# TensorE's queue in the first stage: written order or scheduler's order, in a streaming layer with short convolution and gated delta rule

## The chip, the cores and the metric

The kernel runs on one core of a Trainium2 chip. A core has TensorE (PE, matrix products; its weight loads are shown as PEld), VectorE (DVE), ScalarE (ACT), GpSimd (POOL) and SyncE (SP, which issues the DMAs here). Each engine works through a queue of its own; semaphores tie the queues together. The metric is the device time of one execution in microseconds, as the median of several. Every profile below is of one execution, taken by the hardware profiler.

## The reference

One layer over 4096 new tokens of a prompt (and 32 of a running stream), model width 1024, float32. All tokens are normalised and projected to 4096 columns and 8 gate columns. Mixer A is a gated convolution of width 3 over 512 channels. Mixer B is a gated delta rule with 4 heads of 128, whose state S runs through the whole sequence in chunks:

```python
def hybrid_layer(x, buf_a, buf_qkv, s0, ln_pre, w_in, ...):
    h = rmsnorm(x, ln_pre)
    proj = jnp.einsum('btd,dp->btp', h, w_in)
    b_a, c_a, x_a, z_a, qkv, z_g, a_dec, b_beta = jnp.split(proj, splits, axis=-1)
    conv_a, new_buf_a = causal_dwconv(c_a * x_a, buf_a, conv_a_w)
    y_a = b_a * conv_a * jax.nn.silu(z_a)
    qkv = silu(causal_dwconv(qkv, buf_qkv, conv_qkv_w));  q, k, v = split(qkv)
    q, k = l2norm(heads(q)), l2norm(heads(k));  g, beta = ...
    # gated_delta_rule, by chunks of tokens:
    #   a_mat = strict_lower(kbeta k^T * decay);  t_mat = (I + a_mat)^-1
    #   u = t_mat (v beta);  w = t_mat (kbeta exp(g))
    #   per chunk: v_new = u - w S;  o = (q exp(g)) S + attn v_new
    #              S = S exp(g_last) + k_dec^T v_new
    y_g = rmsnorm_head(o) * silu(z_g)
    return x + rmsnorm_post(concat(y_a, y_g) @ w_out)
```

## The kernel before

The work has three stages. In the first, the 4096 tokens go through in 16 blocks of 256 (two chunks of 128 each), and all of mixer B is done. In the second, mixer A's projections follow in a scheme with fewer products (a_pairs), and in the third the output projection (tiles pjo, go, ro). The change is in the first stage.

**One block of the first stage** has eight pairs of projections on TensorE, in the order c4, c6, c0, c2, c8, c10, z0, z2 (tiles pj_c, pj_z; k, q, v and the gate Z of mixer B). A pair is 48 matmuls (each product in three f16 parts, so 384 a block). A pair's result is evacuated by ScalarE, convolved by VectorE (L436, six instructions) and goes through silu on ScalarE. Between the pairs stand the small pieces:

- norm_qk: transposes of q and k (tile gt, L77), squares on ScalarE (L468), and from them kd on VectorE (L471).
- gram: products of k with k and q (tile gq), evacuated by VectorE to M and at (L490, L491). The 32x32 blocks of M's diagonal go through DRAM: lad (L497) and back to la (L536).
- subst: the triangular inverse of these 32x32 blocks. VectorE starts it (L539 to L541), GpSimd multiplies la by it (L546) and makes 31 steps of a product and a subtraction (L550, L551), VectorE transposes the result (L556), and 16 DMAs on SP spread it to Tc (L560).
- merge, a generator in five pieces: px (M x Tc, tile m), then the products with U, a transpose, and two more products, that put the 64- and 128-wide inverse U together (VectorE L608, ScalarE L620 to L632).
- rec_a and rec_b, generators, once per chunk: a transpose of v (ot), rk and rq (S times k and q; R by VectorE L654, o by ScalarE), rv (U times R; vn by ScalarE L667), rS (S by VectorE L674), mo (o by VectorE L687), then squares on ScalarE (L691), `so` on VectorE (L693, L694), its power -1/2 on GpSimd (L137), the scaling of o (L696, L697), its transposes om and the DMA of mixer B's result.
- gates of the next block (ggate, gcs), and for the second stage prep_a (w_in's columns by DMA L205, VectorE L206, ScalarE L749, GpSimd L750 to L762, DMA out) and prep_t (GpSimd, ScalarE).

**What sets the order.** The program is written by slots: block `gi` has slots from `16*gi` on, two to a pair of projections, and each piece is put into a slot by at_slot. Pieces of a block's merge and recurrence stand up to 44 slots behind the block's first, that is in the next block's pairs and the one after. These pieces are written under high_priority(1500) (the helper `first`). The tile framework's scheduler then makes a queue for each engine by its own times, the priorities and the data that instructions need from each other. On TensorE one thing more holds: the helper class Ordered (its lines L58 to L66) gives, while `on` is set, every matmul and transpose an order dependence on the one written before it:

```python
def queue(self, i):
    ins = getattr(i, "ins", i)
    if self.on and self.last is not None:
        tc.add_manual_dep(ins, self.last.name, ... NoSync ..., reason="order")
    self.last = ins
    return i
```

`T.on` is set from the second block on and taken away when the first stage's slots are done and the second stage's first products are written. Merge's pieces stand at slots 26 and 28 to 31 of their block, the second chunk's recurrence at 31 to 44.

Of the kernel before, what the change touches and what calls it, by code (L numbers as in the profile page):

```python
# [49 lines left out]
def hybrid_kernel(  # L50
# [28 lines left out]
    T = Ordered()  # L79
# [369 lines left out]
    def pair(b, kind, c0):  # L449
        n = b["n"]  # L450
        if kind == "z":
            return z_pair(b, c0)
        if kind == "v":
            return qkv_pair(b, c0, b["v"][:, c0 - 8:c0 - 6, :n])
        h0 = c0 % 4
        return qkv_pair(b, c0, b["qk"][:, h0:h0 + 2, 0 if kind == "k" else 1, :n])
# [253 lines left out]
    def setup_block(b):  # L710
        b["nch"] = b["n"] // b["C"]
        b["qk"] = tl([P, NH, 2, NB1], F32, "qk", 3, b["id"])
        if b["s"]:
            b["v"], b["zg"] = (te([P, NH, NS], F32, x, 1, "s") for x in ("vs", "zgs"))
        else:
            b["v"], b["zg"] = (tl([P, NH, NB1], F32, x, 2, b["id"]) for x in ("v", "zg"))
        b["hist_new"] = te([P, 12, 3], F32, "hists" if b["s"] else "hist", 2 if b["s"] else 3, b["id"])
        b["ss"] = te([P, 2, 2, NH], F32, "ss", 2, b["id"])[:b["C"], :b["nch"]]
        nb = b["C"] // 32
        b["lad"] = dp.tile([2, NH, 4, 32, 32], F32, tag=f"lad{nb}", bufs=2, name=f"lad{b['id']}")[:b["nch"], :, :nb]  # L720
        b["kd"], b["M"], b["at"], b["rec"] = [], [], [], {}
# [12 lines left out]
    def prep_a():  # L734


        i, half = divmod(wa["next"], 2)
        if i >= len(pairs):
            return
        wa["next"] += 1  # L740
        ct = pairs[i][0]
        if not half:
            yield from scaled((ct, ct + 1))
            return
        (a11, a12), (a21, a22) = ((w[:, 0:4], w[:, 4:8]) for w in wa["w"])

        def out(k, src):
            hl = te([P, 2, 4, P], F16, "hl", 4, f"{i}_{k}")
            A.activation(hl[:, 0], src, AF.Copy)  # L749
            G.tensor_tensor(hl[:, 1], src, hl[:, 0], ALU.subtract)  # L750
            dma(wad[i][:, k], hl)

        out(0, a11)
        out(1, a12)
        out(2, a22)
        G.tensor_tensor(a22, a21, a22, ALU.add)
        out(3, a22)
        G.tensor_tensor(a21, a11, a21, ALU.subtract)
        out(5, a21)
        G.tensor_tensor(a11, a22, a11, ALU.subtract)  # L760
        out(4, a11)
        G.tensor_tensor(a12, a12, a11, ALU.subtract)  # L762
        out(6, a12)
# [25 lines left out]
    def prep_t(i):  # L789

        j, k = divmod(i, 4)
        s, d = (te([P, D], F32, "xt", NXT, f"{x}{i}").bitcast(F16).rearrange("p (q x n) -> p q x n", q=4, x=2)
                for x in ("ts", "td"))
        t = te([P, NB1], F32, "hl", 4, f"tt{i}")
        for q in range(4):
            dma(s[:, q], hTd[j][:, q // 2, q % 2, :, k])
        sums(G, *([(v[:, q, 0], v[:, q, 1]) for q in range(4)] for v in (s, d)), t)
        dma(hTt[j][:, :, :, k], d)
# [64 lines left out]
    def at_slot(i, fn, *a):  # L863
        slots.setdefault(i, []).append(lambda: fn(*a))

    def run_slot(i):
        for fn in slots.pop(i, ()):
            fn()
# [6 lines left out]
    def ends(gen):  # L875
        for _ in gen:
            pass

    def finish(p, s0):

        n = p["nch"]
        ra = [rec_a(p, c) for c in range(n)]
        rb = [rec_b(p, c) for c in range(n)]
        mg = merge(p)
        if n == 1:
            for i, g in ((19, ra[0]), (20, ra[0]), (23, mg), (24, ra[0]), (25, ra[0]), (25, rb[0])):
                at_slot(s0 + i, first, next, g, None)
            at_slot(s0 + 30, ends, rb[0])
            at_slot(s0 + 30, out_state, p)
            return  # L890
        for i, g in ((24, ra[0]), (26, ra[0]), (26, mg), (28, mg), (29, mg), (30, mg), (31, mg), (31, ra[1]),
                     (32, ra[0]), (34, ra[0]), (34, rb[0]), (36, ra[1]), (38, ra[1]), (39, rb[0]),
                     (40, ra[1]), (40, rb[1]), (44, rb[1])):
            at_slot(s0 + i, first, next, g, None)
        if p["last"]:
            at_slot(s0 + 41, out_state, p)

    def first_group(grp):

        for b in grp:  # L900
            setup_block(b)
            if b["s"]:
                b["hist"] = te([P, 12, 3], F32, "hists", 2, "i")
                state[1] = te([P, NH, P], F32, "hl", 4, "s0")
                dma(state[1], state_gdn[0, 0].rearrange("h k v -> k h v"))
        for si, (kind, c0) in enumerate(steps):
            if si == 4:
                in_turn([gates(b) for b in grp])
                for b in grp:
                    decays(b)  # L910
            for kd_, c_ in steps[:si + 1 + (AH if si >= AS else 0)]:
                ct = (28 if kd_ == "z" else 16) + c_
                if ct not in W:
                    prep_b(ct)
            if kind != "z":
                init_hist(smp, 16 + c0)
            for b in grp:
                ends(pair(b, kind, c0))
            if si == 6:
                xprep(groups[1][0])  # L920
            if si in (4, 5):
                for b in grp:
                    if si - 4 < b["nch"]:
                        stage1(b, si - 4)
            if si == 5:
                for b in grp:
                    rnorms(b)
                    subst(b)
            if si == 7:
                in_turn([gates(groups[1][0])])  # L930

    prevs = []
    for gi, grp in enumerate(groups):
        b, s0 = grp[-1], 16 * gi
        if gi == 0:
            first_group(grp)
            for p in grp:
                finish(p, s0)
        else:
            T.on = True  # L940
            setup_block(b)
            b["hist"] = prevs[-1]["hist_new"]
            at_slot(s0 + 7, first, norm_qk, b, 0, 0)
            at_slot(s0 + 8, first, norm_qk, b, 1, 0)
            at_slot(s0 + 10, first, norm_qk, b, 0, 1)
            at_slot(s0 + 11, first, gram, b, 0)
            at_slot(s0 + 11, first, norm_qk, b, 1, 1)
            at_slot(s0 + 12, first, gram, b, 1)
            at_slot(s0 + 12, first, rnorms, b)
            at_slot(s0 + 12, first, subst, b)  # L950
            if gi + 1 < len(groups):
                nx = groups[gi + 1][0]
                g = gates(nx)
                at_slot(s0 + 2, xprep, nx)
                at_slot(s0 + 9, next, g)
                at_slot(s0 + 10, next, g)
                at_slot(s0 + 13, ends, g)
            finish(b, s0)
            for si, (kind, c0) in enumerate(steps):
                ps = pair(b, kind, c0)  # L960
                next(ps)
                run_slot(s0 + 2 * si)
                ends(ps)
                run_slot(s0 + 2 * si + 1)
                if si == 3:
                    for _ in range((1 <= gi <= 13) + (gi in (4, 7, 10))):

                        p = prevs[-1]
                        with tc.issue_after(p["subst_end"]):
                            pa = prep_a()  # L970
                            if next(pa, 0) is None:
                                at_slot(s0 + 11, next, pa)
                                at_slot(s0 + 13, ends, pa)
                    if gi in (5, 6, 8, 9, 11, 12, 13, 14):
                        with tc.issue_after(prevs[-1]["subst_end"]):
                            prep_t((5, 6, 8, 9, 11, 12, 13, 14).index(gi))
        if gi + 1 < len(groups):
            decays(groups[gi + 1][0])
        for b in grp:
            if b["last"]:  # L980
                out_hist(b)
        prevs = grp
# [408 lines left out]
```

## Time and profile before

| | us |
|---|---|
| median of 3 runs | 2454.54 (2454.03 to 2456.37) |
| profiled execution | 2458.1 |
| its span | 2456.4 |
| granted TensorE clock, mean | 0.942 |

| engine | busy us | share of the span |
|---|---|---|
| PE | 2150.5 | 88% |
| PEld | 1725.1 | 70% |
| DVE | 1549.1 | 63% |
| POOL | 1335.7 | 54% |
| ACT | 984.2 | 40% |

The profile tells for each instruction its start, its duration, its engine and line, the tiles that it writes and reads, and, in brackets, how long its engine was idle before it and what ended that. The stages lie at 0 to about 1420 us (first), to 2092 (second) and to 2456 (third). A stretch's table of windows shows the busy time of every engine in it with the number of instructions, the granted clock, the DMA engines' share and GB/s.

### The profile page before, as it was taken

The page shows a single profiled execution, that of the slowest core. Times are in us where ns is not written, and L with a number is a line of the kernel's source. Part 1 is how long each engine was busy: PE and PEld are TensorE (multiplying, and loading weights), DVE is VectorE, ACT ScalarE, POOL GpSimd, SP SyncE. Part 2 cuts the span into 40 slices and gives each one's busy share as a digit, 9 for nine tenths or more (in the row PEclk, how much of TensorE's full clock was granted, in tenths as well). Part 3 has the DMA queues.
Part 4 walks back from the last instruction along what each step waited for, and adds up shares of the span by engine and source line. Part 5 has one row for each costly group of instructions (what it writes and reads, how often), then busy time and mean ns, then how long its engine had stood idle before and what let it go on. Part 6 is the DMA issues. An engine that isn't in the chain of part 4 may idle for free. (4 is left out here: it accounts for less than half of the span.)

```text
span 2456.4 us, 48167 instructions
## 1 busy us (share of the span) xinstructions
PE 2150.5 (88%) x18626; PEld 1725.1 (70%) x18626; DVE 1549.1 (63%) x3720; ACT 984.2 (40%) x2513; POOL 1335.7 (54%) x1750
## 2 busy tenths in 40 slices
PE   4667988788888888888989988999999999999998
PEld 3446877677677777777877877878888888544443
DVE  4786766666767686667666654565657456466652
ACT  4454555455545554555555411112221112233331
POOL 3434653657565766477675440274575441476663
PEclk9778999899899989999999999999999999999999
DMA  6344332433333334324241432412121104344432
GB/s 122 45 108 85 81 96 62 87 91 104 78 88 103 95 89 91 102 80 102 73 125 55 130 133 99 158 53 87 44 76 55 52 27 137 117 131 141 150 129 78
DMA packets 257198, 230.81 MB, mean 94 GB/s; under 512 B 111576, under 2 KB 196376, under 8 KB 256968
## 3 DMA queue, kind: packets, MB, share of 16 engines
q1 hardware_dynamic: 256968, 227.73, 33.1%
q8 instruction: 146, 2.39, 0.4%
q14 instruction: 84, 0.69, 0.1%
HBM read 133.09 MB, written 76.74 MB: 85 GB/s over the span
## 5 line engine op out<-in xcount | busy, mean ns | idle before, releaser
L74 PEld LDWEIGHTS <-w 128*128 128x128 f16 x6528 | 640.3, 103 | 139.8 <-POOL w L729 18.4
L74 PE MATMUL pj_c<-hhi,w 128*128 128x256 f16 x3072 | 566.7, 285 | 10.6 <-ACT u L430 10.6
L74 PE MATMUL pj_c<-hlo,w 128*128 128x256 f16 x1536 | 437.8, 285 | 0.0
L74 PEld LDWEIGHTS <-w_a 128*128 128x128 f16 x2880 | 268.0, 98 | 69.1 <-issue 36.0
L74 PEld LDWEIGHTS <-opm 128*128 128x128 f16 x1536 | 149.2, 98 | 176.2 <-issue 0.8
L551 POOL TENSOR_TENSOR lt<-lt 128x112 f32<-128x112 f32 (+29 forms) x496 | 229.2, 462 | 37.8
L550 POOL TENSOR_TENSOR lt<-la,lt 128x112 f32<-128x112 f32 (+29 forms) x496 | 215.0, 433 | 37.3
L436 DVE SCALAR_TENSOR_TENSOR qk<-u,cw,qk 128x256 f32<-128x256 f32 x384 | 217.7, 611 | 23.9 <-ACT qk L434 23.8
L74 PE MATMUL pja<-op,w_a 128*128 128x256 f16 x1536 | 189.7, 273 | 12.3 <-DVE w L1034 5.6
L74 PE MATMUL pj_z<-hhi,w 128*128 128x256 f16 x1024 | 197.9, 291 | 2.0 <-ACT u L430 2.0
L74 PE MATMUL ga<-op,w_a 128*128 128x256 f16 x1152 | 146.4, 274 | 18.4 <-DVE w L1034 11.9
L74 PE MATMUL pj_z<-hlo,w 128*128 128x256 f16 x512 | 148.7, 290 | 0.0
L546 POOL TENSOR_TENSOR la<-la,lt 128x1024 f32<-128x1024 f32 x16 | 37.7, 2355 | 156.4 <-DVE lt L541 103.4
L74 PE MATMUL pjo<-w_o,opm 128*128 128x512 f16 x528 | 118.5, 379 | 0.0
L74 PE MATMUL ro<-w_o,opm 128*128 128x512 f16 x504 | 113.4, 379 | 0.0
L74 PE MATMUL go<-w_o,opm 128*128 128x512 f16 x504 | 113.1, 379 | 0.0
L137 POOL TENSOR_TENSOR oss<-oss,mhalf 128x2 f32<-128x2 f32 (+1 forms) x17 | 50.0, 2941 | 114.7 <-DVE oss L1280 114.7
L1034 DVE TENSOR_TENSOR w<-pja,w 128x256 f32<-128x256 f32 x152 | 61.8, 420 | 72.0 <-PE pja L74 69.9
L750 POOL TENSOR_TENSOR hl<-xtw,hl 128x512 f16<-128x512 f32 x56 | 68.9, 1248 | 61.2 <-ACT hl L749 61.2
L137 POOL TENSOR_TENSOR r<-ss,mhalf 128x16 f32<-128x16 f32 x16 | 49.0, 3060 | 94.9 <-DVE ss L509 80.4
L74 PE MATMUL gq<-qk 128*128 128x256 f32 x256 | 70.2, 410 | 33.2 <-ACT jk L468 31.9
L769 ACT ACTIVATE op<-tsc 128x512 f16<-128x512 f32 x48 | 30.2, 630 | 168.1 <-POOL tsc L775 96.4
(649 smaller groups left out, 4716.3 us busy)
## 6 DMA issues: line engine op xcount, KB each, us to landing
xt<-in_x_prompt_dram SPq DMA_DIRECT2D x32, 512.0 KB
mx<-mxd SPq DMA_DIRECT2D x16, 1024.0 KB
op<-hTd SPq DMA_DIRECT2D x30, 512.0 KB
xtw<-in_w_in_dram SPq DMA_DIRECT2D x28, 512.0 KB
wad<-hl SPq DMA_DIRECT2D x56, 256.0 KB
gB<-gd SPq DMA_DIRECT2D x16, 516.0 KB
hTd<-hhi SPq DMA_DIRECT2D x16, 512.0 KB
hTd<-hlo SPq DMA_DIRECT2D x16, 512.0 KB
```

Of the source, the lines that this page charges most:

```text
L74: return self.queue(nc.tensor.matmul(*a, **k))
L137: G.tensor_tensor(y, x, mhalf[:x.shape[0], :x.shape[-1]], ALU.pow)
L436: V.scalar_tensor_tensor(d, u[:, i, j:j + n], cw[:, j, c0 + i:c0 + i + 1], d, ALU.mult, ALU.add)
L546: E.tensor_tensor(la, la, bc(rl, 1, 32), ALU.mult)
L550: E.tensor_tensor(tm, bc(la[:, j, j + 1:32], 2, w), bc(lt[:, j, 0:w], 1, r), ALU.mult)
L551: last = E.tensor_tensor(lt[:, j + 1:32, 0:w], lt[:, j + 1:32, 0:w], tm, ALU.subtract)
L750: G.tensor_tensor(hl[:, 1], src, hl[:, 0], ALU.subtract)
L769: A.activation(d[i][0], t, AF.Copy)
L1034: V.tensor_tensor(dst, p, src, ALU.add)
```

## The change

One line in the loop over the blocks: the written order of TensorE's queue is no longer asked for. The slots remain as the order in which the program is written, and the pieces under `first` keep their priority.

```diff
@@ -937,7 +937,7 @@
             for p in grp:
                 finish(p, s0)
         else:
-            T.on = True
+            pass
             setup_block(b)
             b["hist"] = prevs[-1]["hist_new"]
             at_slot(s0 + 7, first, norm_qk, b, 0, 0)
```

All engines' queues come out differently. Names carry the block: m7 is the tile of merge of block 7, so6_1 the `so` of block 6's second chunk, pj8_c10 a projection of block 8.

TensorE in block 8's projections, before: rk and rq of block 7's first chunk, both halves of px and gt in one run, inside the pair c10.

```order
L74 MATMUL pj8_c10_10028<-hhi8_8537,w21_26_1441 128x256
L74 MATMUL rk7_0_10053<-S6_1_9905,qk7_8411 128x128 x4
L74 MATMUL rq7_0_10062<-S6_1_9905,qk7_8411 128x128 x4
L74 MATMUL m7_10073<-Tc7_9276,M7_0_9087 32x32 x4
L74 MATMUL m7_10073<-Tc7_9276,M7_1_9173 32x32 x4
L74 MATMUL m7_10073<-Tc7_9276,M7_0_9087 32x32 x4
L74 MATMUL m7_10073<-Tc7_9276,M7_1_9173 32x32 x4
L77 MATMUL gt18_0_10097<-ident_63,qk8_9462 128x128 x4
L74 LDWEIGHTS w22_27_1444
L74 MATMUL pj8_c10_10028<-hhi8_8537,w22_27_1444 128x256
```

TensorE after: the first half of px, in the pair c8.

```order
L74 MATMUL pj8_c8_9875<-hlo8_8538,w18_25_1196 128x256
L74 MATMUL m7_10073<-Tc7_9276,M7_0_9087 32x32 x4
L74 MATMUL m7_10073<-Tc7_9276,M7_1_9173 32x32 x4
L74 LDWEIGHTS w19_25_1197
L74 MATMUL pj8_c8_9875<-hhi8_8537,w19_25_1197 128x256
```

TensorE after: the second half of px, 28 projection matmuls later, in the pair c10 among the gram products of block 8.

```order
L74 MATMUL pj8_c10_10028<-hhi8_8537,w22_27_1444 128x256
L74 MATMUL gq08_0_10149<-qk8_9462 128x256
L74 MATMUL m7_10073<-Tc7_9276,M7_0_9087 32x32 x4
L74 MATMUL m7_10073<-Tc7_9276,M7_1_9173 32x32 x4
L74 MATMUL gq08_0_10149<-qk8_9462 128x256
L74 MATMUL gq18_0_10154<-qk8_9462 128x256 x2
```

The two halves of px are apart now, the first 20 to 26 projections earlier, and rk and rq stand over 100 projections earlier.

GpSimd around the end of block 7's substitution, before: the second `so` of block 6 (so6_1) stands behind the last step and other work.

```order
L551 TENSOR_TENSOR lt7_9199<-lt7_9199 128x8
L750 TENSOR_TENSOR hl4_0_9817<-xtw10_8799,hl4_0_9817 128x512
L750 TENSOR_TENSOR hl4_1_9821<-xtw10_8799,hl4_1_9821 128x512
L750 TENSOR_TENSOR hl4_2_9825<-xtw11_8807,hl4_2_9825 128x512
L542 MEMSET lt8_10249 128x256
L756 TENSOR_TENSOR xtw11_8807<-xtw11_8807 128x512
L544 MEMSET lt8_10249 32x8 x4
L758 TENSOR_TENSOR xtw11_8807<-xtw10_8799,xtw11_8807 128x512
L137 TENSOR_TENSOR so6_1_9916<-so6_1_9916,mhalf_100 128x4
```

GpSimd after: so6_1 among the steps.

```order
L550 TENSOR_TENSOR lt7_9199<-la7_9198,lt7_9199 128x56
L551 TENSOR_TENSOR lt7_9199<-lt7_9199 128x56
L550 TENSOR_TENSOR lt7_9199<-la7_9198,lt7_9199 128x48
L137 TENSOR_TENSOR so6_1_9916<-so6_1_9916,mhalf_100 128x4
L551 TENSOR_TENSOR lt7_9199<-lt7_9199 128x48
L550 TENSOR_TENSOR lt7_9199<-la7_9198,lt7_9199 128x40
L551 TENSOR_TENSOR lt7_9199<-lt7_9199 128x40
```

The second `so` stands six steps ahead of the substitution's end instead of behind it. In the other blocks it stands behind step 22 to 30 of 31.

## Rows read from the trace of the kernel before

**Rows 1.** Windows: us, busy PE, PEld, DVE, ACT, POOL, clock, DMA share, GB/s
```profile
267.00:1340.00 1073.00, 920.90 (x8562) 799.28 (x8561) 730.86 (x1874) 579.16 (x1581) 670.50 (x1137) 0.92 0.35 89
518.00:597.00 79.00, 70.15 (x665) 61.50 (x663) 54.31 (x137) 44.00 (x122) 58.84 (x96) 0.94 0.31 90
566.80:571.00 4.20, 4.15 (x31) 3.43 (x32) 4.20 (x8) 0.37 (x2) 2.66 (x2) 0.50 0.31 106
2092.00:2456.00 364.00, 356.28 (x1717) 168.26 (x1716) 191.66 (x336) 116.55 (x259) 207.72 (x122) 1.00 0.38 125
```

**Rows 2.** Waits: engine, line, waited for: us in total, times, longest
```profile
POOL so L137 <- DVE so L694: 61.3, 13, 18.8
...
PE rv L74 <- DVE R L654: 52.3, 7, 12.2
...
PE gq L74 <- ACT jk L468: 31.9, 13, 4.6
...
PE m L74 <- DMA Tc<-la: 31.0, 11, 4.3
```

**Rows 3.** Timeline, 518 to 598: start, duration, engine, line, out<-in, [idle <-releaser]
```profile
518.33 0.19 DVE L541 TENSOR_TENSOR lt<-lt,bl 128x32 f32<-128x32 f32 x1
...
556.49 0.69 DVE L556 STREAM_TRANSPOSE la<-lt 128x256 f32<-128x256 f32 x1 [1.59 <-POOL lt L551]
...
562.25 0.69 PE L74 MATMUL m<-Tc,M 32*32 32x32 f32 x16
566.85 1.03 PE L74 MATMUL m<-Tc,M 32*32 32x32 f32 x16 [3.92 <-DMA Tc<-la]
...
575.65 1.13 PE L74 MATMUL gq<-qk 128*128 128x256 f32 x4 [1.74 <-ACT jk L468]
...
579.24 1.09 PE L77 MATMUL gt<-ident,qk 128*128 128x128 f32 x4 [2.46 <-DVE at L491]
...
585.28 1.99 PE L74 MATMUL gq<-qk 128*128 128x256 f32 x8
...
597.64 0.19 DVE L541 TENSOR_TENSOR lt<-lt,bl 128x32 f32<-128x32 f32 x1
```

**Rows 4.** Timeline, the first and the last L541 of 14
```profile
266.92 0.19 DVE L541 TENSOR_TENSOR lt<-lt,bl 128x32 f32<-128x32 f32 x1
...
1339.65 0.19 DVE L541 TENSOR_TENSOR lt<-lt,bl 128x32 f32<-128x32 f32 x1
```

**Rows 5.** Timeline of VectorE, a block with w_in's columns
```profile
425.89 0.19 DVE L541 TENSOR_TENSOR lt<-lt,bl 128x32 f32<-128x32 f32 x1
...
460.41 1.32 DVE L206 TENSOR_TENSOR xtw<-xtw,lnp 128x1024 f32<-128x1024 f32 x1 [9.02 <-DMA xtw<-in_w_in_dram]
...
462.87 1.11 DVE L654 SCALAR_TENSOR_TENSOR R<-rk,sm,R 128x128 f32<-128x128 f32 x4
...
476.07 0.68 DVE L556 STREAM_TRANSPOSE la<-lt 128x256 f32<-128x256 f32 x1
```

**Rows 6.** Timeline, the second chunk's R and rv
```profile
539.41 0.27 PE L74 MATMUL pj_c<-hhi,w 128*128 128x256 f16 x1
...
542.91 1.11 DVE L654 SCALAR_TENSOR_TENSOR R<-rk,sm,R 128x128 f32<-128x128 f32 x4
...
544.65 1.06 PE L74 MATMUL rv<-R,U 128*128 128x128 f32 x8
```

**Rows 7.** Timeline, the second chunk's mo, S and `so`, and GpSimd's 25th step
```profile
551.40 0.28 POOL L550 TENSOR_TENSOR lt<-la,lt 128x56 f32<-128x56 f32 x1
...
552.55 1.06 PE L74 MATMUL mo<-vn,at 128*128 128x128 f32 x8
...
557.06 1.08 DVE L674 SCALAR_TENSOR_TENSOR S<-S,E,rS 128x128 f32<-128x128 f32 x4
...
560.66 0.65 DVE L693 TENSOR_TENSOR so<-so,sm 128x4 f32<-128x4 f32 x1 [1.35 <-ACT at L691]
...
563.07 1.01 POOL L137 TENSOR_TENSOR so<-so,mhalf 128x4 f32<-128x4 f32 x1
```

## The prediction

> **What bounds the kernel now.** I read the profile by stretches first. In the first stage's steady part TensorE is busy 920.9 of 1073 us at a granted clock of 0.92, in the last stage 356.3 of 364 at 1.00 [rows 1]. The last stage is full and the change doesn't touch it, so a gain must come out of the first, where some 150 us of idle time and the low clock lie. Second, the table of waits: what TensorE waits for there is R of the recurrence (L654), the squares of norm_qk (L468) and the Tc that the substitution sends through DRAM (L560) [rows 2]. None is large by itself, so I followed one block in the timeline.
>
> It closes a loop [rows 3]. The substitution of a block starts on VectorE with L541 at 518.33 and ends with the transpose L556 at 557.18, 38.9 us later. Tc goes out; the first products of merge (px) start at 562.25, 5.1 us after L556, and the second px wait for the rest of Tc until 566.85 (3.9 us of idle TensorE). In TensorE's written order these px stand ahead of the next block's gram products, and so the last gq is at 587.27, 30.1 us after L556. From there M, the diagonal's way through DRAM and back, and L541 at 597.64 take 10.4. Nothing of the next substitution can start earlier, and none of the three legs has slack: 38.9 + 30.1 + 10.4 = 79.3. The loop runs 13 times from 266.92 to 1339.65 [rows 4], 82.5 us a turn. Six turns are like this one. In the seven others w_in's columns are prepared, L206 waits in VectorE's queue for its DMA, R and L556 stand behind it, and L541 to L556 takes up to 50.9 us (425.89 to 476.75) [rows 5].
>
> So the stage ends when the loop has turned, and what the change is worth is: by how much it shortens L556 to the last gq, less what it adds inside the substitution.
>
> **The change part by part.** *TensorE, L556 to the last gq.* Counted in projection matmuls from a block's start, the first half of px moves from 264 to about 238, the second half stays at 264 or goes to 280, the gq move from 288 and 312 to 262 to 312, gt from 192 and 216 to 103, and the first rk/rq from 264 to 139 to 170. So px no longer waits for all of Tc in a row: while the second half's DMA is under way there are 26 or more projections to run, and gt and rk are gone from this stretch. The walk, with the durations of the rows: one projection is (544.65 - 539.41)/48 = 0.109 us, from the first behind rq to rv [rows 6]. Between the first px and the last gq stand 73 of them, 8.0 us; px's second half 1.0, one gt 1.1, sixteen gq twice 1.1 and 2.0, 4.2 [rows 3], the gates' products an estimated 0.8 and the first products with U an estimated 0.9 (32 small ones; px's 32 take 0.7 and 1.0): 16.0. The first px still come at L556 + 5.1, since the DMA sets that, and last 0.7. After an idle stretch of that kind TensorE runs at half clock: 0.50 in the 4.2 us behind the wait for Tc [rows 1], which loses 2.1. Sum: 5.1 + 0.7 + 16.0 + 2.1 = 23.9 instead of 30.1: **-6.2 a turn**. Bounds: -8 if the clock holds; -3 if the waits for the squares and for M's buffers (1.7 and 2.5 in this block) both come back in full.
>
> *GpSimd.* The rsqrt of the second chunk's norm (`so`, L137) took its turn after the 31 steps of the substitution; it now stands behind step 22 to 30. It takes 1.0 us [rows 7], all of it on the loop: **+1.0**. Some 18 steps of prep_t get ahead of later substitutions; at GpSimd's mean of 670.5/1137 = 0.6 us [rows 1] that is 11 us over 13 turns: **+0.8**, between 0 and 1.
>
> *Is `so` there in time?* In this block mo ends at 553.61, 35.3 us after L541, and its `so` runs at 563.07 [rows 7]. In between S (L674) stood behind L556 in VectorE's queue (557.06); in the new order S, o and `so` stand ahead of L556. Unblocked, the rows give S 1.1, o 0.7, the squares 1.4 and the two `so` steps 0.8: 4.0. mo comes about 86 projections earlier relative to the block, of which 6 go to the earlier gq: 35.3 - 80 x 0.109 = 26.6, and with `so`'s 4.0 it is ready at 30.6 plus what TensorE waits in the recurrence. GpSimd reaches its place (551.40 is the 25th step) at 33.1 [rows 7]. The spare is 2.5 us. I take the wait as 0, with 0 to 9 as its range; this is the choice on which the forecast hangs.
>
> *The recurrence's covers on TensorE.* Between rk and rv of the second chunk stood 48 projections, now 24; rv to rS 48, now 22; rS to rk 48, now 26. Twenty-four are 2.6 us. In this block R was finished at 544.02, 4.6 us after the end of rk and rq [rows 6], mostly behind convolutions on VectorE; in the new order R stands directly behind `so`'s steps. So each link may wait 0 to 2.5 us; I take 2.5 for all of them. They lie beside the substitution, not on it, as long as TensorE is at px when Tc is: TensorE is busy 70.2 us in a turn of 79 [rows 1], so a turn of 74.9 still leaves 4.8.
>
> *The seven turns with L206.* R and the first chunk's `so` now stand ahead of L206 in five of them, which may save what the first `so` waited; but the second chunk's S and `so` now stand behind the second L206, which started at 460.41, 34.5 us after its L541 [rows 5], and behind that the substitution's last steps on GpSimd. A few us each way; I take 0, between -4 and +8.
>
> *Start and end.* In the block after the first, the last gq falls back from 312 to 400: 88 x 0.109 = 9.6 us, partly caught up in the next block: **+8**, between 0 and 13. The second stage's start is interleaved otherwise; no row prices it, 0, between -5 and +5. The other engines' queues keep their work and cost nothing by themselves, since the loop hides all that isn't named here.
>
> **Sum:** 13 x (-6.2 + 1.0 + 0.8) = -57, + 8 = -49. The profiled execution took 2458.1 us (span 2456.4), 3.6 above the median of 2454.5: 2458.1 - 49 = 2409, as a median **2405.5**.
>
> **Rivals.** (A) *`so` holds up the substitution.* GpSimd takes its instructions in order: in before it waited 61.3 us in 13 waits for `so`, and whatever stood behind it waited too [rows 2]. Now a part of the substitution itself stands behind the second one. For it: the spare is 2.5 us only, the covers are halved, so that TensorE's waits (up to 2.5 on each of four links) push mo back; and where L206 waits, `so` comes at about 34.5 + 1.3 + 4 and some convolutions, 42, against GpSimd's arrival at 33. Against it: VectorE's order has been eased at just this place. Price: 7 us a turn (half of the turns 9, half 5) is 13 x 7 = +91, so -49 + 91 = +42: **2496**. It decides from 49/13 = 3.8 us of wait a turn on; above that the kernel is slower than before.
>
> The Trainium skill, PSUM — Partial Sum Buffer, section "Engine vs sequencer instructions", says that the queues of ScalarE, VectorE and GpSimdE are strictly first in, first out. It speaks for (A): by it no step of the substitution overtakes a waiting `so`. The trace agrees (the 13 waits above); how late `so` is, the page can't tell.
>
> (B) *TensorE becomes the bound.* If each link waits its 2.5 and the squares' waits return, 8 to 9 us in all, TensorE's 70.2 and these make 78.7 a turn: hardly under 79.3, and in the other turns the gain is still there in part. 7 x -4.4 + 8 = -23 at best, 0 at worst: 2431 to 2455, middle **2443**. For it: the halved covers. Against: R and S have moved ahead in VectorE's queue too.
>
> (C) *More than forecast.* The turns with L206 lose 4 us each as well (7 x 4 = 28) and the start costs nothing: -49 - 28 - 8 = -85: **2369.5**. For it: 52.3 us of waits for R [rows 2], all in such turns. Against: the second chunk's `so` behind L206.
>
> (D) *The change moves little.* Excluded by the order: nearly every piece moves.
>
> **How the numbers follow.** Forecast 2380 to 2430: 0.38. (A) 0.32. (B) 0.18, a third of it within 0.2% of 2454.5 (2449.6 to 2459.4, about what a measurement of this kernel can tell from no change). (C) 0.12. Faster 0.38 + 0.12 + 0.12 = 0.62, same 0.06, slower 0.32. The range takes in (C) and (A) up to 8 us a turn (2509): 2355 to 2508; the forecast's own is 2380 to 2430.
>
> **What would show it.** Right: L556 to the last gq at 24 us or less, no idle time of 3 us or more ahead of the second px, L541 to L556 at 39 to 41 in turns without L206, a period near 78. Wrong by (A): waits of the substitution's L550/L551 rows behind `so`, L541 to L556 at 45 or more everywhere, waits for `so` on GpSimd well above 61 us. Wrong by (B): waits on TensorE for R, vn and S on every turn and px late against Tc. It would also be wrong if Tc's DMAs, which share SP's queue and the DMA engines with more transfers at once, landed later than 5 us after L556.

## The result

| | us |
|---|---|
| kernel before, median of 4 runs | 2454.28 (2445.64 to 2456.37) |
| changed kernel, median of 4 runs | 2385.59 (2383.20 to 2391.97) |
| ratio | 0.9731, 95% interval 0.9701 to 0.9761 |
| span of the profiled execution, before and after | 2456.4 and 2384.1 |

The changed kernel is 68.7 us faster by the medians; 49 were forecast. The size came out near, but the experiments show that a part of the reasoning behind it doesn't hold.

The profile's first part for the changed kernel: TensorE does the same 18626 matmuls in 9 us less busy time, and its share rises from 88% to 90%.

```profile
PE 2141.4 (90%) x18626; PEld 1713.9 (72%) x18626; DVE 1564.8 (66%) x3720; ACT 980.3 (41%) x2513; POOL 1333.7 (56%) x1750
```

Windows of the changed kernel: the loop's 13 turns (first to fourteenth L541), then two stretches behind the first stage. The columns are those of [rows 1].

```profile
265.46:1290.91 1025.45, 907.48 (x8481) 780.33 (x8480) 739.55 (x1865) 571.70 (x1571) 664.05 (x1135) 0.94 0.36 93
...
1390.00:1428.00 38.00, 36.66 (x390) 32.17 (x388) 20.53 (x51) 5.90 (x14) 2.54 (x2) 1.00 0.06 19
1428.00:1468.00 40.00, 40.00 (x368) 36.40 (x367) 24.35 (x63) 6.55 (x26) 3.15 (x3) 1.00 0.55 194
```

And of the kernel before, the same 13 turns and the stretches that answer to the two:

```profile
266.92:1339.65 1072.73, 920.63 (x8560) 799.04 (x8559) 730.75 (x1873) 579.16 (x1581) 670.43 (x1136) 0.92 0.35 89
...
1442.00:1480.00 38.00, 32.02 (x339) 27.75 (x339) 21.52 (x54) 6.75 (x24) 1.43 (x1) 1.00 0.07 19
1480.00:1520.00 40.00, 34.90 (x307) 30.74 (x305) 19.52 (x55) 8.02 (x30) 4.54 (x4) 1.00 0.09 28
```

The 13 turns (a turn is from one L541 to the next) shrink from 1072.7 to 1025.5 us, 47.3 in all: 34 us less idle time of TensorE (152.1 to 118.0) and 13 us less busy time. Most of these 13 us are not the clock: 79 fewer matmuls fall into the window, since 84 more had run before the loop's first L541 (1803 against 1719). They are missing in the first turn, which shrinks from 78.6 to 65.0 us. In the twelve turns behind it the matmuls are equal in number (7906 and 7907), and the time falls from 994.2 to 960.5: 30 us less idle time, 3.6 less busy time at a clock of 0.94 instead of 0.92. Behind the loop TensorE is idle less as well. By the times of the L541 rows the 72.3 us of span fall into four parts:

| stretch | before | after | difference |
|---|---|---|---|
| start to the first L541 of the loop | 266.9 | 265.5 | -1.5 |
| 13 turns | 1072.7 | 1025.5 | -47.3 |
| one more, shorter turn | 67.8 | 64.0 | -3.7 |
| last L541 to the end | 1049.0 | 1029.2 | -19.8 |

With the first turn counted to the start, these are 15 us at the start, 34 in twelve turns (2.8 a turn) and 24 at the end.

What TensorE waits for in the 13 turns has changed altogether (waits of the changed kernel: us in total, times, longest):

```profile
PE gt L77 <- ACT qk L437: 29.5, 24, 3.8
PE om L77 <- DVE o L697: 25.3, 12, 7.0
PE ot L77 <- DVE zg L703: 17.0, 8, 5.3
PE rk L74 <- DVE S L674: 12.9, 8, 8.7
PE rS L74 <- ACT vn L667: 12.3, 5, 4.1
...
PE rv L74 <- DVE R L654: 4.3, 3, 3.2
PE m L74 <- DMA Tc<-la: 2.7, 4, 1.0
```

The three waits on which the argument rested were 52.3 us for R, 30.3 for the squares and 30.0 for Tc in the 13 turns of the kernel before ([rows 2] are of its whole execution). They are down to 4.3, nothing and 2.7. In their place stand 97 us of waits for silu, o, zg, S and vn, none of which the kernel before has in these turns.

A turn without L206 in the changed kernel, of the kind of [rows 3] (in the turn of that very block, from 502.6 on, the last gq comes 26.6 us after L556):

```profile
980.72 0.19 DVE L541 TENSOR_TENSOR lt<-lt,bl 128x32 f32<-128x32 f32 x1
...
1014.66 1.01 POOL L137 TENSOR_TENSOR so<-so,mhalf 128x4 f32<-128x4 f32 x1
...
1019.31 0.69 DVE L556 STREAM_TRANSPOSE la<-lt 128x256 f32<-128x256 f32 x1 [0.68 <-POOL lt L551]
...
1023.73 0.68 PE L74 MATMUL m<-Tc,M 32*32 32x32 f32 x16
...
1029.87 0.69 PE L77 MATMUL gt<-ident,qk 128*128 128x128 f32 x2 [3.84 <-ACT qk L437]
...
1036.11 0.69 PE L74 MATMUL m<-Tc,M 32*32 32x32 f32 x16
...
1045.63 1.03 PE L74 MATMUL gq<-qk 128*128 128x256 f32 x4
...
1058.97 0.19 DVE L541 TENSOR_TENSOR lt<-lt,bl 128x32 f32<-128x32 f32 x1
```

The two halves of px (1023.73 and 1036.11) run without a wait; the second is 12 us later than the first. `so` comes in the middle of the substitution without a wait. But the last gq ends at 1046.66, 26.7 us after L556, not 24: TensorE now waits 3.84 us for the silu of q before gt, and runs at half clock behind that (granted clock 0.50 from 1029.87 to 1034.50). Not every wait has that price: behind this turn's shorter ones, 0.68 to 1.46 us, the granted clock stayed at 1.00.

The legs of a turn, as means of the 13 turns, worked out from the rows of L541, L556 and the last gq. They stand here for the later runs too:

| kernel | L541 to L556 | L556 to the last gq | last gq to L541 | turn |
|---|---|---|---|---|
| before | 42.6 | 30.1 | 9.8 | 82.5 |
| changed | 43.8 | 23.7 | 11.4 | 78.9 |
| `so` behind the substitution | 43.2 | 25.5 | 10.9 | 79.5 |
| L206 behind L556 | 41.3 | 24.7 | 11.2 | 77.1 |
| before, 10 steps left out | 35.4 | 37.1 | 9.7 | 82.3 |
| changed, 10 steps left out | 35.8 | 32.8 | 10.8 | 79.4 |
| x loads behind la | 44.5 | 25.6 | 10.5 | 80.6 |
| px by hand | 41.8 | 33.1 | 9.7 | 84.6 |
| recurrence and gt by hand | 44.0 | 29.9 | 10.4 | 84.3 |
| both by hand | 44.5 | 31.8 | 9.4 | 85.8 |

How far one execution differs from another shows in the next run, the end alone: in the 13 turns its four engines' queues are in the same order as in the kernel before, yet they take 1064.5 us instead of 1072.7, with legs of 41.8, 30.2 and 9.9. So a difference of 0.8 us in such a mean is not clear of chance, nor one of 1.5 us in that of the seven turns with L206 (86.4 and 84.9).

### The profile page after: what moved, and what is told of

Read it like the earlier page. It is cut to its first block, busy times and chain, and to the rows that moved or that the text cites. A ratio compares the mean times of both kernels' runs of the same rounds, so it can differ in the third digit from the quotient of the medians.

```text
span 2384.1 us, 48173 instructions
## 1 busy us (share of the span) xinstructions
PE 2141.4 (90%) x18626; PEld 1713.9 (72%) x18626; DVE 1564.8 (66%) x3720; ACT 980.3 (41%) x2513; POOL 1333.7 (56%) x1750
## 5 line engine op out<-in xcount | busy, mean ns | idle before, releaser
L74 PEld LDWEIGHTS <-w 128*128 128x128 f16 x6528 | 624.8, 101 | 117.7 <-POOL w L729 16.9
L74 PE MATMUL pj_c<-hhi,w 128*128 128x256 f16 x3072 | 559.6, 282 | 3.0 <-ACT u L430 3.0
L551 POOL TENSOR_TENSOR lt<-lt 128x112 f32<-128x112 f32 (+29 forms) x496 | 235.4, 475 | 37.0
L436 DVE SCALAR_TENSOR_TENSOR qk<-u,cw,qk 128x256 f32<-128x256 f32 x384 | 238.5, 667 | 9.5 <-ACT qk L434 9.1
L74 PE MATMUL pj_z<-hhi,w 128*128 128x256 f16 x1024 | 187.9, 281 | 0.0
L74 PE MATMUL ga<-op,w_a 128*128 128x256 f16 x1152 | 147.7, 274 | 10.5 <-DVE w L1034 6.7
L769 ACT ACTIVATE op<-tsc 128x512 f16<-128x512 f32 x48 | 30.2, 630 | 173.0 <-POOL tsc L775 100.0
L436 DVE SCALAR_TENSOR_TENSOR v<-u,cw,v 128x256 f32<-128x256 f32 x192 | 98.6, 549 | 3.0 <-ACT v L434 2.8
L437 ACT ACTIVATE qk<-qk 128x512 f32<-128x512 f32 x64 | 40.2, 633 | 142.8 <-DVE qk L436 142.8
```

The costliest lines, as they stand in the source:

```text
L74: return self.queue(nc.tensor.matmul(*a, **k))
L436: V.scalar_tensor_tensor(d, u[:, i, j:j + n], cw[:, j, c0 + i:c0 + i + 1], d, ALU.mult, ALU.add)
L437: queued("silu", lambda: A.activation(dst, dst, AF.Silu))
L551: last = E.tensor_tensor(lt[:, j + 1:32, 0:w], lt[:, j + 1:32, 0:w], tm, ALU.subtract)
L769: A.activation(d[i][0], t, AF.Copy)
```

## The experiments

All medians are compared with runs of the kernel before on the same chip.

### The end alone, and the blocks alone

```diff
+    T.on = False
     early.close()
```

That is the kernel before with the written order given up behind the loop over the blocks.

> The blocks of the first stage keep TensorE's written order; only from the end of the loop over the blocks on (the last blocks' remaining slots, written between the second stage's first products) is it left to the scheduler. The changed kernel needed 20 us less from the last L541 on. If that belongs to the order of these pieces: 2430 to 2440 us. If it was left behind by the blocks (TensorE further ahead when the loop ends): 2450 to 2456 us.

Measured: 2426.2 against 2454.4 us, ratio 0.9894 (0.9873 to 0.9915), 28 us faster and a little below the range expected for that; from the last L541 on it needed 1023.3 us instead of 1049.0. TensorE's windows there are as full as in the changed kernel:

```profile
1430.00:1468.00 38.00, 36.65 (x390) 32.12 (x388) 19.50 (x45) 6.01 (x14) 3.33 (x6) 1.00 0.06 19
1468.00:1508.00 40.00, 40.00 (x368) 36.47 (x367) 25.53 (x67) 7.21 (x27) 3.65 (x3) 1.00 0.45 154
```

The counterpart is the changed kernel with `T.on = True` put at the same place.

> The counterpart of the run with the end only: the blocks of the first stage are left to the scheduler as in the changed kernel, and the written order holds again from the end of the loop over the blocks on. If the end's share is separate (the run with the end only took 25 us off from the last L541 on): 2405 to 2412 us, with the loop's period as in the changed kernel, 78.9. If the end was gained in the blocks already: 2385 to 2390 us.

Measured: 2413.6 against 2451.2, ratio 0.9843 (0.9824 to 0.9862). The turn is 79.1, as in the changed kernel, and from the last L541 on it takes 1052.4. The two shares, 28.2 and 37.6, add up to 65.8 of 68.7. So 23 to 26 us by the traces (from the last L541 on: 1052.4 to 1029.2, 1049.0 to 1023.3), 28 by the medians, belong to the order in which the last blocks' pieces stand between the second stage's first products, and have nothing to do with the loop. In the written order they cost idle time of TensorE; the scheduler's order fills it.

### The first two blocks

```diff
-            T.on = True
+            T.on = gi <= 2
```

> The changed kernel, but TensorE keeps the written order in the first two of the blocks in the loop (blocks 1 and 2). In the changed kernel the third L541 of the loop came 15 us earlier than before, of which 5 to 6 would be the turns' usual gain. If the start's order was worth the rest: 2392 to 2398 us. If what is held back there is made up later: 2384 to 2388 us. By the prediction's term for the start (+8 for the gram products that fall back in block 1) it would be faster, about 2377 us.

Measured: 2397.9 against 2451.2, ratio 0.9777 (0.9760 to 0.9793), and 12 us more than the changed kernel's median. In the trace the fourth L541 of the stage comes at 429.7, against 413.7 in the changed kernel and 425.9 before; from there to the end it takes 1970.6, the changed kernel 1970.4. So the freedom in the first two blocks alone is worth 16 us of trace, 12 by the medians. The forecast had put +8 there.

### The same pieces moved by hand

Three kernels keep the written order and move pieces by slots to about where the scheduler put them. The first parts px:

```diff
+            if q == 0:
+                yield
...
-        for i, g in ((24, ra[0]), (26, ra[0]), (26, mg), (28, mg), (29, mg), (30, mg), (31, mg), (31, ra[1]),
+        for i, g in ((24, ra[0]), (25, mg), (26, ra[0]), (27, mg), (28, mg), (29, mg), (30, mg), (31, mg), (31, ra[1]),
```

> TensorE's written order is kept as in the kernel before; only the first half of px stands one slot earlier and the second half one slot later. Theory 1 (the two halves of px in one run are what costs, since everything behind them waits for all of Tc): L556 to the last gq falls from 30 to about 24 us, 13 turns x -6 = -78, 2375 to 2395 us. Theory 2 (what counts is how much of TensorE's work is left between L556 and the last gq; gt, rk and rq still stand there, and TensorE is no further on when L556 ends): the wait for the second half's Tc (3.9 us) is only replaced by one for the first, 0 to -2 us a turn, 2428 to 2455 us.

Measured: 2485.6 against 2454.4, ratio 1.0127 (1.0108 to 1.0147), slower than either theory. The waits between 267 and 1340 us:

```profile
PE gq L74 <- ACT jk L468: 40.4, 12, 4.7
PE m L74 <- DVE o L689: 25.7, 6, 6.8
...
PE m L74 <- DMA Tc<-la: 13.5, 5, 5.1
```

The wait for Tc halves (30 to 13.5), but the squares are waited for longer, and a new wait appears: px's tile `m` has one buffer, which the mo of the chunk before uses too, and px one slot earlier must wait until VectorE has read mo (o, L689 in this kernel). The last gq comes at 33.1 after L556, not 24: px taken apart is not enough. Whether px in front of the gram products is what delays them, as the forecast has it, this run can't tell, since the wait for `m` came in with the edit.

The second moves the recurrence (covers of 24) and gt:

```diff
-((24, ra[0]), (26, ra[0]), ... (32, ra[0]), (34, ra[0]), (34, rb[0]), (36, ra[1]), (38, ra[1]), (39, rb[0]), (40, ra[1]), (40, rb[1]), (44, rb[1]))
+((20, ra[0]), (22, ra[0]), ... (32, ra[0]), (33, ra[0]), (33, rb[0]), (34, ra[1]), (35, ra[1]), (36, rb[0]), (36, ra[1]), (36, rb[1]), (40, rb[1]))
-at_slot(s0 + 7, first, norm_qk, b, 0, 0);  at_slot(s0 + 8, first, norm_qk, b, 1, 0)
+at_slot(s0 + 4, first, norm_qk, b, 0, 0);  at_slot(s0 + 5, first, norm_qk, b, 1, 0)
```

> TensorE's written order is kept; by hand the pieces of the recurrence are written earlier (covers of 24 projections instead of 48, so that rk and rq of the next block's first chunk stand before the turn's end) and the first two gt too, about where the changed kernel has them; px stays in one run at its old slot. Theory 1: TensorE only comes to px earlier and waits longer for Tc, L556 to the last gq stays at 28 to 30; the second chunk's so now stands inside the substitution (+1 a turn): 2440 to 2475 us. Theory 2 (less work left behind L556 is the gain): -4 us a turn and +1: 2410 to 2420 us. A third, that the early recurrence by itself is the gain (R is waited for 52 us in all): 2400 us or less.

Measured: 2496.7, ratio 1.0187 (1.0158 to 1.0216), slower than all three theories. R's wait is gone (0.9 us), yet o and zg are now waited for, 44.4 and 31.3 us. The third joins both.

> TensorE's written order is kept; the recurrence's pieces and gt early as in the run with these alone, and px's halves apart as in the run with these alone. If the loop's gain is the order of these pieces and no freedom is needed: L556 to the last gq 23 to 25, 13 turns x (-6 + 1 to 2 for the so inside the substitution) = -50 to -65, no gain at the start and at the end: 2390 to 2405 us. If it takes the scheduler's finer interleaving (pieces one by one between projections): waits for R, S and vn come back, 2420 us or more.

Measured: 2518.7, ratio 1.0269 (1.0250 to 1.0288). Its waits in the same stretch:

```profile
PE om L77 <- DVE o L699: 52.9, 7, 12.2
PE gq L74 <- ACT jk L468: 38.4, 12, 4.6
PE gt L77 <- DVE at L491: 34.3, 12, 4.5
PE ot L77 <- DVE zg L705: 17.1, 6, 9.8
PE rv L74 <- ACT U L634: 12.0, 13, 1.3
```

With nearly the positions of the changed kernel, counted in slots, the written order is 133 us slower than the scheduler's; some 28 of them, by the run on the end, come from the end, where the written order was kept too. So the coarse positions that the prediction counted don't bring the gain by themselves. What is left is the places between the slots (pieces stand matmul by matmul between projections) and the other queues, which the scheduler makes anew together with TensorE's. Which of the two weighs more wasn't separated, so for the loop the cause of the gain is open to that extent.

### What stands inside the substitution

The changed kernel with the second chunk's rsqrt put behind the last step:

```diff
+            with tc.issue_after(nxt["subst_end"]):
+                rsqrt(so[:, 0], f)
...
```

> The changed kernel, but the second chunk's rsqrt (so on GpSimd) stands behind the last step of the substitution that runs meanwhile. In the changed kernel it costs 1.0 us a turn and in the turns with L206 GpSimd waits 0 to 8.5 us for it. If these lie on the loop: L541 to L556 falls by 1 in six turns and by 3 to 5 in seven, -25 to -40 us: 2345 to 2360 us. If TensorE bounds the turn by now (70 of 79 us busy and half clock behind each wait), L556 comes earlier and px waits for TensorE: 2375 to 2387 us. Slower if o and om, which wait for so, then hold TensorE's queue.

Measured: 2390.9 against 2451.2, ratio 0.9753 (0.9738 to 0.9768); against the changed kernel's 0.9731 no gain, and above both ranges. L541 to L556 falls by 0.7, which isn't clear of chance, and L556 to the last gq grows by 1.8. What `so` does is seen in a turn with L206 of the changed kernel:

```profile
413.74 0.19 DVE L541 TENSOR_TENSOR lt<-lt,bl 128x32 f32<-128x32 f32 x1
...
446.80 1.23 DVE L206 TENSOR_TENSOR xtw<-xtw,lnp 128x1024 f32<-128x1024 f32 x1 [10.01 <-DMA xtw<-in_w_in_dram]
...
455.25 1.01 POOL L137 TENSOR_TENSOR so<-so,mhalf 128x4 f32<-128x4 f32 x1 [8.48 <-ACT u L430]
...
462.53 0.21 POOL L551 TENSOR_TENSOR lt<-lt 128x8 f32<-128x8 f32 x1
462.77 0.69 DVE L556 STREAM_TRANSPOSE la<-lt 128x256 f32<-128x256 f32 x1 [0.30 <-POOL lt L551]
```

VectorE stands at L206 until 446.80, 33 us after L541; S and `so` queue behind it; GpSimd waits 8.5 us for `so` (the row names ScalarE's u; `so`'s own last step on VectorE, L694, ended at 455.10) with the rest of the substitution behind that. The same turn with `so` behind the last step (L541 at 412.14):

```profile
453.62 0.20 POOL L551 TENSOR_TENSOR lt<-lt 128x8 f32<-128x8 f32 x1
...
463.19 0.67 DVE L556 STREAM_TRANSPOSE la<-lt 128x256 f32<-128x256 f32 x1
```

The substitution ends 7 us earlier, but VectorE is still busy with what queued up behind L206, and L556 comes no sooner. As means of the seven turns with L206, the last step ends 42.6 us after L541 instead of 46.5, and L556 ends 4.0 us behind it instead of 0.8. So rival (A)'s mechanism exists and costs the substitution 3.8 us in such a turn; taken away alone it gives nothing, since VectorE's queue holds L556 for as long.

The cause behind it taken away: L206 behind L556 of the running substitution.

```diff
-                        with tc.issue_after(p["subst_end"]):
+                        with tc.issue_after(p["subst_end"]), tc.issue_after(p["tr_end"]):
```

> The changed kernel, but L206, which waits in VectorE's queue for w_in's DMA, stands behind L556 of the substitution that runs meanwhile, so that R, S, so and L556 have nothing of it ahead of them. If L206 is what makes the substitution 46 us long in seven turns instead of 39: 7 x -5 to -7 = -35 to -50, 2335 to 2350 us. If TensorE bounds the turns: a part of it only, 2360 to 2380 us. If the columns' own work, started later, falls into the next substitution on GpSimd: 2385 us or more.

Measured: 2364.7 against 2451.2, ratio 0.9645 (0.9628 to 0.9661), 21 us less than the changed kernel.

```profile
407.50 0.19 DVE L541 TENSOR_TENSOR lt<-lt,bl 128x32 f32<-128x32 f32 x1
...
446.60 0.69 DVE L556 STREAM_TRANSPOSE la<-lt 128x256 f32<-128x256 f32 x1 [1.09 <-POOL lt L551]
447.18 1.58 DVE L206 TENSOR_TENSOR xtw<-xtw,lnp 128x1024 f32<-128x1024 f32 x1
```

In the turns with L206, L541 to L556 falls from 47.2 to 41.9 us, the whole excess but 1.4. Of these 5.3 us, 3.8 come back in L556 to the last gq (23.5 to 27.2); such a turn goes from 82.5 to 80.8. The other six turns gain 1.9 each, though nothing in them was edited; the scheduler made their queues anew too.

### Ten steps of the substitution left out

```diff
-        for j in range(31):
+        for j in range(21):
```

The inverse stays incomplete; sizes, DMAs and products are the same. This measures the disputed leg itself, in both kernels.

> The kernel before with the last 10 of the substitution's 31 steps left out (the inverse is then incomplete, so its values are not the reference's; all sizes, DMAs and products stay). The 10 steps took about 6.5 us in each turn. If the loop through the substitution sets the turn as the prediction has it: -3.9 (the wait for Tc that goes) to -6.5 us in 13 turns and about as much in the three others, 2355 to 2405 us. If TensorE's own chain sets it: above 2430 us.

Measured: 2452.5 against 2450.9, ratio 1.0011 (0.9999 to 1.0022): no change, where the prediction's loop asked for -50 to -100.

> The changed kernel with the same 10 steps left out. If the substitution still sets the turn: -6.5 us in 13 to 16 turns, 2280 to 2305 us. If TensorE sets it by now (70 of 79 us busy, half clock behind each wait): L556 comes 6 us earlier and L556 to the last gq grows by nearly as much, -0 to -2 us a turn, 2355 to 2385 us.

Measured: 2399.8 against 2450.9, ratio 0.9786 (0.9767 to 0.9806), 14 us slower than the changed kernel and outside both ranges. In both, L541 to L556 is 7 to 8 us shorter (in the kernel before the last step ends 8.6 us earlier, and L556 stands 1.4 us longer behind it) and L556 to the last gq 7 to 9 us longer. A turn of the shortened kernel before, TensorE first:

```profile
566.15 1.09 PE L74 MATMUL m<-Tc,M 32*32 32x32 f32 x32
...
570.29 1.03 PE L74 MATMUL gq<-qk 128*128 128x256 f32 x4
579.54 2.07 PE L74 MATMUL gq<-qk 128*128 128x256 f32 x4 [8.23 <-ACT jk L468]
...
587.06 1.99 PE L74 MATMUL gq<-qk 128*128 128x256 f32 x8
```

px no longer waits at all: L556 came at 550.4, its start is 15.7 us later. But gq waits 8.23 us for the squares. Why, ScalarE's rows tell:

```profile
573.34 0.63 ACT L437 ACTIVATE v<-v 128x512 f32<-128x512 f32 x1 [5.49 <-DVE v L436]
573.97 1.28 ACT L329 ACT_TABLE_LOAD   x1
...
577.94 0.26 ACT L468 ACTIVATE jk<-gt 128x128 bf16<-128x128 f32 x1
```

gt was done at 568, yet ScalarE stood at the silu of v, which waited for VectorE's convolution, and behind that stood the gates' table load; the squares came ten us later. The waits between 267 and 1340 us show that this took over from Tc and more:

```profile
PE gq L74 <- ACT jk L468: 68.4, 13, 8.2
PE rv L74 <- DVE R L654: 48.7, 8, 13.0
```

TensorE's idle time in the 13 turns, its span less its busy time, is the same with the steps and without: 152.1 and 157.7 us before, 118.0 and 118.8 in the changed kernel.

```profile
268.82:1338.19 1069.37, 911.71 (x8562) 793.16 (x8561) 759.40 (x1873) 584.18 (x1581) 587.87 (x876) 0.92 0.35 89
```

One reservation: the scheduler made the other queues anew for the shorter substitution (in the kernel before VectorE's and ScalarE's, with TensorE's order kept; in the changed kernel TensorE's too), and ScalarE's order above is a result of that. A shorter substitution with every queue left as it was has not been tried.

The trace of the kernel before tells a part of it without any edit. In the turn of [rows 3], this is the stretch from the end of the last gq of the block before to the first px:

```profile
508.46:562.25 53.79, 53.05 (x521) 47.81 (x518) 34.39 (x87) 28.88 (x81) 37.43 (x75) 1.00 0.31 82
```

TensorE was busy for 53 of 53.8 us, at full clock; in each of the six turns without L206 it was idle for no more than 0.8 us there. So the substitution ran beside a full TensorE, and a shorter one could give back little more than the wait for Tc behind the first px (30.0 us in the 13 turns) and the clock lost behind it. With the ten steps left out px came at the same time of the turn, 48.5 us after L541, as the second px had before: no longer held by Tc, but by TensorE's own work and by new waits for zg and kd (2.02 and 0.58 us).

### The last leg

The x loads of a later block stand, in several turns of the changed kernel, just ahead of la on SP (1050.62 in the turn above, la at 1051.74). This run puts them behind it.

```diff
-            dma(xt[:m], src[b["o"] + t0:b["o"] + t0 + m, :])
+            with tc.issue_after(la_end[0]) if la_end[0] else ExitStack():
+                dma(xt[:m], src[b["o"] + t0:b["o"] + t0 + m, :])
```

> The changed kernel, but the loads of a later block's x stand behind the way back of the diagonal (la) on SP; in the changed kernel they were issued just ahead of it in several turns, and the last gq to L541 took 11.4 us instead of 9.8. If these loads are what delays la: 11.4 falls to about 9.8, -10 to -21 us, 2365 to 2376 us. If TensorE sets the turn, or the order of M's two halves on VectorE makes the difference: 2383 to 2388 us.

Measured: 2406.1 against 2450.9, ratio 0.9809 (0.9791 to 0.9827), 20 us slower than the changed kernel and outside both ranges. The leg itself does shrink, to 10.5 (in the six turns without L206 from 10.9 to 9.7), but the other two grow by 2.5 together, and the fourth L541 of the stage is 6.5 us later. Both edits together:

> The changed kernel with L206 behind L556 (from the second block of the loop on, so that the first isn't held back as in the run before, where its turn took 7 us more) and with the x loads behind la. If the two add: 2364.7 - 7 - 10 = 2345 to 2355 us. If TensorE sets the turn by then: 2355 to 2362 us.

Measured: 2365.0 against 2450.9, ratio 0.9643 (0.9625 to 0.9660), the same as with L206 alone and a little above both ranges. The two fastest kernels of this study are these, at 0.964.

## Why the prediction was right, and where it was not

- **Sum and sign.** 2405.5 was forecast, 2385.6 came. The parts did not come as forecast: 13 turns -57 forecast, -47.3 measured; start and end together +8 forecast, -25 measured. With the first turn counted to the start it is plainer: -2.8 a turn instead of -4.4 in twelve turns, -15 at the start and -24 at the end. The errors of the parts cancel in part, so that the sum came this near is partly luck.
- **L556 to the last gq.** Forecast -6.2 a turn, measured -6.4 as a mean. The walk behind it was right only in part: px hardly waits for Tc any more (30.0 to 2.7 us), gt and rk are gone from the stretch; but in a turn like [rows 3] it is 26.7 and not 23.9, since gt now waits for the silu of q. The mean is reached by the turns with L206 (30.1 to 23.5) and by the first turn, 15.0, which belongs to the start.
- **GpSimd.** Forecast +1.8, measured +1.2 on L541 to L556. In turns without L206 `so` is in time behind the first turn, as chosen (1014.66, no wait; in the loop's first two turns the second chunk's stands behind all 31 steps), and the leg's mean rises from 38.5 to 39.9. In those with L206 it was 46.1 and is 47.2. The forecast's 0 for them came near, but as the sum of two things that it hadn't: waits for `so` let the last step end 46.5 instead of 41.2 us after L541, and L556, which before ended 4.9 us behind that step in VectorE's queue, now ends 0.8 behind it.
- **The last leg** was forecast unchanged and cost 1.6 us a turn: in the turn above la lands 6.6 us after its issue, behind x loads that now stand ahead of it, against 4.3 in that of [rows 3]. The run with these loads behind la gives 0.9 of the 1.6 back, which is little more than chance. This edit of SP's queue had not been walked.
- **The start: wrong step.** "88 x 0.109 = 9.6 us" took a gram product that falls back in block 1 as time lost. It was time in which TensorE ran projections that before had waited in line: 84 more matmuls were done at the loop's first L541, which came no later (265.5 against 266.9), and the first turn shrinks from 78.6 to 65.0. By the run with the order kept there it is worth 12 us (medians) to 16 (traces). A piece that moves back is a loss only if nothing useful moves ahead of it.
- **The end: wrong step.** "No row prices it, 0, between -5 and +5" left out that TensorE was idle for 5 to 6 us in each 40 behind the first stage; the window rows of before (32.0 of 38, 34.9 of 40) showed it. Both runs on it give 23 to 28 us.
- **"None of the three legs has slack": wrong.** This is the step that failed most. That each block's L541 follows the last one by three legs is true of any periodic schedule; it doesn't say that the legs bind. The trace of before has it already: in the turns without L206 the substitution runs beside a TensorE that is idle for no more than 0.8 us (508.46:562.25 above), so only the wait for Tc and the clock lost behind it could be won there. Ten steps less changed nothing, with the reservation above, since TensorE then waited for zg, kd and above all ScalarE's squares instead of Tc. The wait for the squares stood in [rows 2] with the same 31 us as that for Tc; the two were near a tie, and the prediction followed one. What the change gave shows as less idle time of TensorE all over the stage; the path through the substitution itself, L541 to L556, did not get shorter.
- **The rivals.** (A) happened in size in the turns with L206 (waits of up to 8.5 us for the second chunk's `so`, and one of 10.6 for a first chunk's), but hardly in price, since L556 lost its wait in VectorE's queue. The 61.3 us of [rows 2] that it was measured against are of the whole execution; in the 13 turns all waits of GpSimd for `so` were 28.9 us before and are 47.5. (B) is the nearest to what was found: S and vn are waited for, 12.9 and 12.3 us, and what is gained in one leg is lost to TensorE's queue in another; its price, 2443, is far off. Of (C) the start that costs nothing came true. The turns with L206 lost 3.9 us in all, where (C) asked for 8.4; another edit, L206 behind L556, gave 1.6 more, hardly clear of chance.

## What to carry to other kernels

A chain that closes from block to block is not yet the bound: before building a sum on a leg, look whether another engine is busy all along beside it, and whether a second wait of the same size stands behind the one that would go; if a run is to be had, leave out some of the leg's work. Moving pieces by hand to where a scheduler put them may bring the opposite of its gain: here one shared buffer (px and mo) turned a shorter wait into a longer one, and in the run with fewer steps one in-order queue did (the squares behind a silu). Behind a stage that is changed, its first and last blocks deserve their own walk: here they gave more than half of the gain (28 and 12 of 69 us by the medians).

## What was not expected

An instruction that waits for a DMA in the middle of an in-order queue cost more than its own engine shows: L206, some 30 us after L541 in seven turns, held S, `so` and through it the substitution on GpSimd; put behind L556 it waits for nothing (447.18), and the kernel is 21 us faster with the same work. And TensorE's clock is a part of the gain: over the whole execution its busy time for the same 18626 matmuls fell from 2150.5 to 2141.4 us as the mean granted clock rose from 0.942 to 0.956, and to 2134.6 at 0.962 in the run with L206 behind.
